# Turning the FFN's input rows: identity products on TensorE replaced by 16-bit halves turned by DMA and summed on POOL, with a new order of an SSD chunk's steps

## The chip, the core and the metric

One core of a Trainium2 chip runs the whole layer in one launch. TensorE (PE) multiplies, DVE (VectorE), ACT (ScalarE) and POOL (GpSimd) do the elementwise work, SP (SyncE) issues nearly all DMAs, in the order of its queue. The metric is the device time of one execution in microseconds (us), lower is better; the median of repeated runs is compared.

## What is computed

One decoder layer on 2048 rows of 1024 numbers (float32):

```python
h = x + rms_norm(W_out @ [SSD(groupA); RWKV7(groupB)], post_mix_norm)   # both read rms_norm(x, pre) @ w_in
hn = rms_norm(h, pre_ffn_norm)
u = causal_conv(hn @ ffn_w_up)                    # 2 x 2816 columns
y = h + rms_norm((silu(gate) * val) @ ffn_w_down, post_ffn_norm)
```

The SSD mixer works in 16 chunks of 128 rows with a state carried from chunk to chunk:

```python
y_diag = (C B^T * decay_in) X ; y_off = C state_in * exp(a_cs) ; state = decay * state + B^T (decay_states X)
y = group_rms_norm((y_diag + y_off + D x) * silu(z)) * norm_g
```

## The kernel before

The program has three phases. Phase R (to about 1010 us) computes the RWKV half and the input products for both halves. Phase S computes the SSD half chunk by chunk, multiplies both halves by `w_out`, adds `x`, writes `h` to memory (`H`), normalises it for the FFN and writes it *transposed* to memory (`HN`, features on partitions, 1024 tokens in each of two tensors). Phase F is the FFN in two halves of 1024 tokens: up products with weights split in two 16-bit halves (a factored form with seven products for eight), convolution, gate and down products. The first half also makes the split weights and stores them to memory (`UW`, `DW`); the second half loads them.

**Who sets the order.** On PE the order is that of the program text throughout. On the other engines and on SP's queue, in phase S and for the FFN's first two column blocks, the framework's scheduler lists the instructions by a simulation of the program. From then on `Program` (L56) writes the order for DVE, ACT, POOL and SP: it keeps a list of operations with an estimated length and the operations they depend on, plays PE's order forward, gives each other operation a due time, and picks on each engine the ready operation that is due first. `Q` is SP's queue. An operation on `Q` that writes no tile of the plan is a store (`UW<-w` L1344, `DW<-dw` L1580, the output rows L1710).

**A round of phase S.** `S_PLAN` is the order of the steps of one round n (1 to 15); `c` is chunk n, `n` chunk n+1, `p` chunk n-1, `q` chunk n-2, `s` and `t` the next pair of chunks, in even and in odd rounds. PE executes them in this order:

- `c.begin` (L947): identity products of X (`px`) and the scores (`psc`); DVE makes `Xdt` and `yt`.
- `c.decay.g` (L978): two products make a bank `bc` from `R` (rows of running decays, fetched by `n.rows`, L974, after `t.flip`, L909, has written them to memory); four ACT exponentials, then DVE and ACT take the rest. There is one `bc` bank.
- `Z` (L931): one quarter of a later chunk's `z` product, 6 matmuls; after the fourth quarter ACT copies the bank (`sz<-z`, L943). There is one such bank. Three `Z` of a round are used in rounds 1 to 12 and four in 13 to 15 (`S_QUOTA`).
- `c.off`, `c.keys`, `c.y`, `c.state`: the state's part `pf` (its scratch on DVE has the tag `sq`), the turned keys `pb`, the chunk's own part `py` with the gate and the norm's squares (scratch `sq`), and the new state `pst`.
- `p.norm` (L1040): four identity products turn the normalised rows (`pY`); ACT and DVE make the two 16-bit halves `Y`.
- `p.o.dh.part` (L1050): 12 matmuls of half `dh` of the output product; part 0 reads `yr` (RWKV's rows), part 1 reads `Y`. After part 1 ACT copies the bank to `m`. There are two `o` banks.
- `q.post.0` and `q.post.1` (L1070): the square of `m` and its root, `m` times the gain, plus `x` on POOL, store to `H`, square and root again, `xi` = normalised rows times the gain (DVE, L1085). Then for each half of 512 features four identity products turn `xi` into a bank `ht` that shares the two `o` banks (L1090), ACT copies it into `hT`, and after the second half one DMA stores `hT` to `HN`. The first half of `hT` serves as scratch for the squares.
- `s.steps`, `t.sums`, `t.flip`: step sizes and running decays of the next pair.

After round 15 the tail (`S_TAIL`) interleaves the last chunks' steps with the FFN's first two column blocks (`F`).

Of the kernel before, what the change touches and what calls it, by code (L numbers as in the profile page):

```python
# [7 lines left out]
F32 = mybir.dt.float32  # L8
F16 = mybir.dt.float16
BF16 = mybir.dt.bfloat16  # L10
AF = mybir.ActivationFunctionType
ALU = mybir.AluOpType
# [5 lines left out]
D = 1024  # L18
P = 128
KT = 8  # L20
# [35 lines left out]
class Program:  # L56

    SHARED = 0.55, 0.75  # L60
    LAG = {"T": 0.25, "V": 0.12, "A": 0.14, "G": 0.12, "Q": 2.0}

    def __init__(self):
        self.on, self.ops, self.writer, self.readers, self.tensor, self.near = False, [], {}, {}, None, set()

    def add(self, engine, us, fn, reads=(), writes=()):
        if not self.on:
            fn()
            return
        n = len(self.ops)  # L70
        before = set()
        for r in reads:
            if r in self.writer:
                before.add(self.writer[r])
            self.readers.setdefault(r, []).append(n)
        for w in writes:
            if w in self.writer:
                before.add(self.writer[w])
            before.update(self.readers.pop(w, ()))
            self.writer[w] = n  # L80
        if engine == "T":
            if self.tensor is not None:
                before.add(self.tensor)
            self.tensor = n
        if engine == "V" and any(r[0] in ("u", "d") for r in reads):
            self.near.add(n)
        before.discard(n)
        self.ops.append((engine, us, fn, before))

    def run(self):  # L90
        ops = self.ops
        count = len(ops)
        after = [[] for _ in ops]
        for n, (_, _, _, before) in enumerate(ops):
            for b in before:
                after[b].append(n)
        due, at = [1e9] * count, 0.0
        for n, (engine, us, _, _) in enumerate(ops):
            if engine == "T":
                due[n] = at  # L100
                at += us
        for n in range(count - 1, -1, -1):
            engine, us, _, _ = ops[n]
            for a in after[n]:
                due[n] = min(due[n], due[a] - us - self.LAG[engine])
        left = [len(o[3]) for o in ops]
        ready = [0.0] * count
        wait = {k: [] for k in self.LAG}
        for n in range(count):
            if not left[n]:  # L110
                wait[ops[n][0]].append(n)

        now, order, busy, coming = 0.0, [], {}, []
        while len(order) < count or busy:
            for k, some in wait.items():
                if k in busy:
                    continue
                some = [n for n in some if ready[n] <= now + 1e-9]
                if some:
                    n = min(some, key=lambda n: (due[n], n))  # L120
                    wait[k].remove(n)
                    order.append(n)
                    busy[k] = [ops[n][1], n]
            rate = dict.fromkeys(busy, 1.0)
            if "V" in busy and "G" in busy and busy["V"][1] not in self.near:
                rate["V"], rate["G"] = self.SHARED
            step = min([v[0] / rate[k] for k, v in busy.items()] + [
                ready[n] - now for k, some in wait.items() if k not in busy for n in some])
            now += step
            for k in list(busy):  # L130
                busy[k][0] -= step * rate[k]
                if busy[k][0] < 1e-9:
                    n = busy.pop(k)[1]
                    for a in after[n]:
                        ready[a] = max(ready[a], now + self.LAG[k])
                        left[a] -= 1
                        if not left[a]:
                            wait[ops[a][0]].append(a)
        for n in order:
            ops[n][2]()  # L140
        self.__init__()


class Space:
# [27 lines left out]
    "Dt", "pp rr ones3 E", "identb mnegb", "Btok", "Xdt", "Xd", "aend dec sgs sgv sgr", "ST0 ST1", "sq", "yt0",  # L172
)
S_RIGHT = (
    "ident_s mhalf_s", "ssm pov por ss pnv pnr", "Y", "yr", "xi", "m", "gpost", "gpre2", "hT", "yt", "wo",
)
F_EARLY = ("us", "s3", "b0", "b1", "b2", "b3")
F_MID = (
# [8 lines left out]
c.decay.1 m.z.2 m.z.3 t.steps u.z.0 u.z.1 u.z.2 n.rows c.y u.z.3 c.state  # L187
"""
S_PLAN = """
c.begin c.decay.0 Z c.off p.norm c.keys Z c.decay.1 p.o.0.0 Z t.sums s.steps p.o.0.1 t.flip Z n.rows q.post.0 c.y c.state  # L190
p.o.1.0 q.post.1 p.o.1.1
"""
S_QUOTA = (3,) * 12 + (4,) * 3
S_TAIL = """
# [46 lines left out]
def bcast_row(tc, K, pool, i, name):  # L241
    t = pool.tile([P, D], F32, name=name)
    tc.nc.scalar.dma_start(t, K.rows[i].partition_broadcast(P))
    return t
# [14 lines left out]
def rsqrt_cols(tc, K, pool, ss, n, scale, eps, name, psum=False, bufs=1):  # L259

    nc = tc.nc
    v = pool.tile([P, n], F32, name=name + "v", tag=name + "v", bufs=bufs)
    r = pool.tile([P, n], F32, name=name + "r", tag=name + "r", bufs=bufs)
    (nc.vector if psum else nc.gpsimd).tensor_scalar(out=v, in0=ss, scalar1=scale, scalar2=eps, op0=ALU.mult, op1=ALU.add)  # L264
    nc.gpsimd.tensor_tensor(out=r, in0=v, in1=K.mhalf[:, :n], op=ALU.pow)  # L265
    return r
# [518 lines left out]
def phase_S(tc, K, x, w_z, w_dt, w_o, XN, XC, YR, H, HN, blocks=8):  # L785
    nc = tc.nc
    V, S, G_ = nc.vector, nc.scalar, nc.gpsimd
    TB = 256
    wk, psp = Space(tc, "s_"), Space(tc, "sp_", space=PSUM)
# [50 lines left out]
    def bank(name, tag, bufs=1):  # L840
        return psp.tile([P, 4, P], F32, name=name, tag=tag, bufs=bufs)
# [81 lines left out]
    class Chunk:  # L923
# [146 lines left out]
        def post(self, part):  # L1070

            m, n = self.m, self.n
            if part == 0:
                ss = wk.tile([P, 1], F32, name="ssm" + self.cf, tag="ssm")
                self.hT = wk.tile([P, KT, P], F32, name="hT" + self.cf, tag="hT")
                jk = self.hT.rearrange("p a b -> p (a b)")[:, 0:D // 2].bitcast(BF16)
                S.activation(jk, m, AF.Square, accum_out=ss)
                r = rsqrt_cols(tc, K, wk, ss, 1, 1.0 / D, EPS, "po")
                V.scalar_tensor_tensor(out=m, in0=m, scalar=r[:, 0:1], in1=gpost, op0=ALU.mult, op1=ALU.mult)
                G_.tensor_tensor(out=m, in0=m, in1=self.xin, op=ALU.add)  # L1080
                K.marks[n] = nc.sync.dma_start(H[n], m)
                ss = wk.tile([P, 1], F32, name="ssh" + self.cf, tag="ss")
                S.activation(jk, m, AF.Square, accum_out=ss)
                r = rsqrt_cols(tc, K, wk, ss, 1, 1.0 / D, EPS, "pn")
                V.scalar_tensor_tensor(  # L1085
                    out=self.xin, in0=m, scalar=r[:, 0:1], in1=gpre2, op0=ALU.mult, op1=ALU.mult)
            ps = (bank(f"ht{self.cf}{part}", "yb") if n >= N - 2 else bank(f"ht{self.cf}{part}", "o", 2))
            for u in range(4):
                kt = 4 * part + u
                nc.tensor.transpose(ps[:, u, :], self.xin[:, kt * P:(kt + 1) * P], K.ident)  # L1090
            S.activation(self.hT[:, 4 * part:4 * part + 4, :], ps, AF.Copy)
            if part == 1:
                nc.sync.dma_start(HN[n // 8][:, :, P * (n % 8):P * (n % 8) + P], self.hT)


    N = 2 * blocks
# [45 lines left out]
    gpost = bcast_row(tc, K, wk, 1, "gpost")  # L1142
    gpre2 = bcast_row(tc, K, wk, 2, "gpre2")
# [759 lines left out]
```

## Time and profile before

| | |
|---|---|
| median of 3 runs (lowest, highest) | 2685.07 us (2680.1, 2686.81) |
| profiled execution | 2684.99 us, its span 2682.6 us |
| mean granted PE clock | 0.972 of full speed |
| busy: PE, DVE, ACT, POOL | 2470.8 (92%), 1925.8 (72%), 1210.7 (45%), 1223.3 (46%) us |
| rounds 2 to 15 of phase S | 1036 to 1376 us |
| tail, FFN's first half, second half | 1376 to 1434, to 2082, to the end |

The span runs from the first to the last instruction of the profiled execution. A busy time is the sum of an engine's instructions. A wait is put down to the instruction that released it; idle time of an engine that is not the bound costs nothing.

### The profile page before, as it was taken

Reading aid. Unit: us, or ns where it says so; the run is one execution under the profiler, and the core shown is the slowest. Engines: PE = TensorE matmul, PEld = TensorE weight load, DVE = VectorE, ACT = ScalarE, POOL = GpSimd, SP = SyncE. Lnnn points to the kernel's source line nnn. Section 1 sums busy time; section 2 is a strip of 40 time slices with the busy share of each in tenths; the row PEclk is TensorE's granted clock in tenths of the full one; section 3 lists DMA queues with packets and bytes.
Section 4 is the critical chain, followed back from the end, with each engine's and each line's share of the span. In section 5 each row is a group of like instructions: output and inputs, shape, how many; then the busy total and the mean of one; then the engine's idle time right before and its main releaser. Section 6 shows DMA issues by size and latency. Waiting matters only on the chain. (4 is left out here: it accounts for less than half of the span.)

```text
span 2682.6 us, 53962 instructions
## 1 busy us (share of the span) xinstructions
PE 2470.8 (92%) x21340; PEld 1554.9 (58%) x21340; DVE 1925.8 (72%) x3655; ACT 1210.7 (45%) x2467; POOL 1223.3 (46%) x1324
## 2 busy tenths in 40 slices
PE   4889999999999988999997999999998999999998
PEld 4778888888888855555543344444433444444443
DVE  7768777777777665567777868787889836565557
ACT  6445555555565453444444543435353333123132
POOL 2344444444545343224467565556657523222135
PEclk8899999999999989999999899999999999999999
DMA  7233222332223253334355444343435643333243
GB/s 211 71 66 71 53 60 58 67 78 53 56 60 71 78 176 110 107 124 136 128 194 169 155 143 153 130 173 114 168 115 192 196 140 100 103 102 102 87 151 112
DMA packets 309341, 310.74 MB, mean 116 GB/s; under 512 B 168160, under 2 KB 213600, under 8 KB 305760
## 3 DMA queue, kind: packets, MB, share of 16 engines
q1 hardware_dynamic: 307792, 305.72, 37.8%
q8 instruction: 167, 2.74, 0.4%
q10 hardware_dynamic: 1296, 1.58, 0.2%
q14 instruction: 86, 0.70, 0.1%
HBM read 187.85 MB, written 110.99 MB: 111 GB/s over the span
## 5 line engine op out<-in xcount | busy, mean ns | idle before, releaser
L1375 PE MATMUL u<-b,w 128*128 128x512 f16 x3696 | 815.2, 383 | 32.2 <-ACT w L1216 15.9
L1375 PEld LDWEIGHTS <-w 128*128 128x128 f16 x3696 | 363.3, 99 | 480.5 <-issue 27.8
L286 PE MATMUL d<-xt,wr 128*128 128x129 f16 x5376 | 336.8, 224 | 17.0 <-DMA xt<-xh 15.3
L1611 PE MATMUL d<-dw,fa 128*128 128x512 f16 x1512 | 336.9, 381 | 12.8 <-DVE dw L1575 10.6
L286 PEld LDWEIGHTS <-wr 128*128 128x128 f16 x5376 | 322.9, 100 | 30.6 <-ACT wr L249 15.3
L1611 PEld LDWEIGHTS <-fa 128*128 128x128 f16 x1596 | 157.2, 98 | 213.5 <-issue 30.5
L1393 DVE TENSOR_TENSOR C<-u,C 128x512 f32<-128x512 f32 x220 | 150.5, 685 | 155.7 <-PE u L1375 148.9
L286 PE MATMUL c<-xt,wc 128*128 128x131 f16 x3072 | 205.2, 227 | 24.1 <-ACT tr L426 10.8
L286 PEld LDWEIGHTS <-wc 128*128 128x128 f16 x3072 | 189.0, 100 | 40.7 <-issue 32.4
L1624 DVE TENSOR_TENSOR acc<-d,acc 128x512 f32<-128x512 f32 x212 | 139.9, 682 | 50.8 <-PE d L1611 50.0
L573 DVE TENSOR_TENSOR tmp<-atl,xl 128x60 f32<-128x60 f32 (+24 forms) x465 | 140.5, 302 | 44.0 <-DMA atl<-ATd 32.5
L1428 DVE SCALAR_TENSOR_TENSOR p<-C,fpar,p 128x1024 f32<-128x1024 f32 x88 | 128.4, 1459 | 60.5 <-ACT p L1424 58.1
L1223 DVE SCALAR_TENSOR_TENSOR w<-us,w 128x512 f16<-128x512 f32 x132 | 121.5, 927 | 53.8 <-ACT w L1216 51.0
L1221 POOL TENSOR_TENSOR fa<-p,fa 128x512 f16<-128x512 f32 x100 | 132.6, 1342 | 58.2 <-ACT fa L1216 58.1
L449 DVE SCALAR_TENSOR_TENSOR ca<-rc,cw,ca 128x128 f32<-128x128 f32 x384 | 132.5, 390 | 25.6 <-POOL ca L444 25.3
L1216 ACT ACTIVATE fa<-p 128x512 f16<-128x512 f32 x110 | 66.5, 626 | 152.6 <-DVE p L1441 125.3
L576 DVE TENSOR_TENSOR xl<-xl,tmp 128x60 f32<-128x60 f32 (+24 forms) x465 | 124.4, 268 | 11.2
L1434 POOL COPY fcarry<-C 128x2 f32<-128x2 f32 x88 | 35.4, 402 | 197.0 <-DVE C L1393 196.9
L1428 DVE SCALAR_TENSOR_TENSOR a<-C,fpar,a 128x1024 f32<-128x1024 f32 x88 | 115.3, 1310 | 7.4 <-ACT a L1424 5.4
L1347 POOL TENSOR_TENSOR us<-us,us 128x512 f32<-128x512 f32 x66 | 101.4, 1536 | 41.2 <-DMA us<-in_w_u_dram 20.7
L1389 ACT ACTIVATE C<-u 128x512 f32<-128x512 f32 x88 | 51.9, 590 | 143.7 <-PE u L1375 126.4
L1216 ACT ACTIVATE w<-us 128x512 f16<-128x512 f32 x132 | 80.0, 622 | 78.1 <-POOL us L1347 57.1
(316 smaller groups left out, 4495.5 us busy)
## 6 DMA issues: line engine op xcount, KB each, us to landing
UW<-w SPq DMA_DIRECT2D x154, 256.0 KB
w<-UW SPq DMA_DIRECT2D x154, 256.0 KB
us<-in_w_u_dram SPq DMA_DIRECT2D x88, 256.0 KB
DW<-dw SPq DMA_DIRECT2D x70, 256.0 KB
dw<-DW SPq DMA_DIRECT2D x56, 256.0 KB
hs<-HN SPq DMA_DIRECT2D x48, 256.0 KB
r<-in_w_d_dram SPq DMA_DIRECT2D x10, 1024.0 KB
xin<-in_x_dram SPq DMA_DIRECT2D x16, 512.0 KB
```

Source lines behind the costliest of these rows:

```text
L286: nc.tensor.matmul(ps, w[:, a, kt, :], xt[:, b, kt, cols], start=n == 0, stop=n == 3 * KT - 1)
L449: V.scalar_tensor_tensor(out=acc[:, q], in0=raw[:, q, k:k + 128], scalar=cw[:, g + q, k:k + 1], in1=acc[:, q], op0=ALU.mult, op1=ALU.add)
L573: chain.tensor_tensor(out=tmp[:, :m, :n], in0=atl[:, j, j + 1:32].unsqueeze(1).to_broadcast([P, m, n]), in1=xl[:, :m, j:j + 1].to_broadcas ...
L576: chain.tensor_tensor(out=xl[:, :m, j + 1:32], in0=xl[:, :m, j + 1:32], in1=tmp[:, :m, :n], op=ALU.add)
L1216: S.activation(h, src, AF.Copy, **({} if scale is None else {"scale": scale}))
L1221: {"V": V, "G": G_}[engine].tensor_tensor(out=l, in0=src, in1=h, op=ALU.subtract)
L1223: V.scalar_tensor_tensor(out=l, in0=src, scalar=scale, in1=h, op0=ALU.mult, op1=ALU.subtract)
L1375: nc.tensor.matmul(bk[at], self.w[i][:, u, k, :], self.half.b[i][:, k, v, :], start=start and n == 0, stop=n == 11, skip_group_check=True)
L1393: op("V", .61, lambda: V.tensor_tensor(out=part(j, x), in0=bk[at], in1=part(*a), op=ALU.add), (("u", 4 * s + at), (*(c0, c1)[a[0]], a[1])) ...
L1428: V.scalar_tensor_tensor(out=o[j], in0=C[j][:, 2 - d:1026 - d], scalar=cw[:, g, 2 - d:3 - d], in1=o[j], op0=ALU.mult, op1=ALU.add)
L1611: nc.tensor.matmul(bk[s, t], pairs[m].a[i][:, u, t * P:t * P + P], pairs[m].w[n][0][:, v, :], start=new and m == 0 and u == v == 0, stop=m ...
L1624: V.tensor_tensor(out=acc[j][:, t], in0=bk[s, t], in1=acc[j][:, t], op=ALU.add)
```

## The change

`post` no longer uses PE. For each half of 512 features ACT converts `xi` to 16 bits (`hl`), DVE subtracts that from `xi` and leaves the 16-bit rest in `xi`'s own place, two DMAs from SP's queue transpose both halves into `tu`, POOL adds them to float32 (`hT`, now half as large), and one DMA stores that half to `HN`. The squares' scratch becomes the tag `sq` (in the last two chunks `yt`). The steps of a round have a new order: `c.off` follows the first decay, two `Z` stand side by side, `q.post.0` follows the second decay and `q.post.1` follows `t.sums`, and `c.y` and `c.state` move behind `p.o.1.0`. In the planner a store becomes ready 4 us later than what it waits for.

```diff
+    STORE = 4.0
     LAG = {"T": 0.25, "V": 0.12, "A": 0.14, "G": 0.12, "Q": 2.0}
...
+        if engine == "Q" and not writes:
+            self.far.add(n)
...
-                        ready[a] = max(ready[a], now + self.LAG[k])
+                        ready[a] = max(ready[a], now + self.LAG[k] + self.STORE * (a in self.far))
...
-    "ident_s mhalf_s", "ssm pov por ss pnv pnr", "Y", "yr", "xi", "m", "gpost", "gpre2", "hT", "yt", "wo",
+    "ident_s mhalf_s", "ssm pov por ss pnv pnr", "Y", "yr", "xi", "m", "gpost", "gpre2", "hT", "hl", "tu", "yt", "wo",
...
 S_PLAN = """
-c.begin c.decay.0 Z c.off p.norm c.keys Z c.decay.1 p.o.0.0 Z t.sums s.steps p.o.0.1 t.flip Z n.rows q.post.0 c.y c.state
-p.o.1.0 q.post.1 p.o.1.1
+c.begin c.decay.0 c.off Z Z c.decay.1 Z q.post.0 p.norm Z c.keys p.o.0.0 t.sums q.post.1 s.steps p.o.0.1 t.flip n.rows
+p.o.1.0 c.y c.state p.o.1.1
 """
...
-                self.hT = wk.tile([P, KT, P], F32, name="hT" + self.cf, tag="hT")
-                jk = self.hT.rearrange("p a b -> p (a b)")[:, 0:D // 2].bitcast(BF16)
+                jk = wk.tile([P, D], BF16, name="jk" + self.cf, tag="sq" if n < N - 2 else "yt", bufs=1 if n < N - 2 else 2)
...
-            ps = (bank(f"ht{self.cf}{part}", "yb") if n >= N - 2 else bank(f"ht{self.cf}{part}", "o", 2))
-            for u in range(4):
-                kt = 4 * part + u
-                nc.tensor.transpose(ps[:, u, :], self.xin[:, kt * P:(kt + 1) * P], K.ident)
-            S.activation(self.hT[:, 4 * part:4 * part + 4, :], ps, AF.Copy)
-            if part == 1:
-                nc.sync.dma_start(HN[n // 8][:, :, P * (n % 8):P * (n % 8) + P], self.hT)
+            cs = slice(512 * part, 512 * part + 512)
+            hi = wk.tile([P, 512], F16, name=f"hl{self.cf}{part}", tag="hl", bufs=2)
+            S.activation(hi, self.xin[:, cs], AF.Copy)
+            lo = self.xin[:, 512 * part:512 * part + 256].bitcast(F16)
+            V.tensor_tensor(out=lo, in0=self.xin[:, cs], in1=hi, op=ALU.subtract)
+            tu = wk.tile([P, 2, 4, P], F16, name=f"tu{self.cf}{part}", tag="tu")
+            nc.sync.dma_start_transpose(tu[:, 0], hi)
+            nc.sync.dma_start_transpose(tu[:, 1], lo)
+            hT = wk.tile([P, 4, P], F32, name=f"hT{self.cf}{part}", tag="hT")
+            G_.tensor_tensor(out=hT, in0=tu[:, 0], in1=tu[:, 1], op=ALU.add)
+            nc.sync.dma_start(HN[n // 8][:, 4 * part:4 * part + 4, P * (n % 8):P * (n % 8) + P], hT)
```

## Rows read from the trace of the kernel before

**Rows 1.** Busy time by stretch: us, each engine (instructions), granted clock, DMA share, GB/s

```profile
1036.00:1222.00 186.00, 177.95 (x1069) 103.43 (x1068) 115.39 (x230) 78.80 (x220) 60.25 (x72) 1.00 0.35 115
1222.00:1376.00 154.00, 143.57 (x780) 80.82 (x779) 112.92 (x175) 73.61 (x194) 73.34 (x76) 0.96 0.46 148
1376.00:1434.00 58.00, 49.45 (x224) 23.04 (x222) 46.22 (x41) 28.41 (x47) 42.47 (x35) 0.91 0.60 201
1434.00:2082.00 648.00, 598.37 (x2682) 264.06 (x2681) 536.40 (x606) 291.19 (x456) 394.92 (x327) 0.97 0.44 150
```

**Rows 2.** PE in order of time, one odd round: start, us, line, out<-in [idle before]

```profile
1105.78 0.60 PE L955 MATMUL px<-ident_s,xbc 128*128 128x128 f32 x4
...
1109.46 0.60 PE L1045 MATMUL pY<-ident_s,yt 128*128 128x128 f32 x4
...
1116.08 2.75 PE L1065 MATMUL o<-wo,Y 128*128 128x512 f16 x12
...
1120.06 0.66 PE L1090 MATMUL ht<-ident_s,xi 128*128 128x128 f32 x4 [1.12 <-DVE xi L1085]
...
1120.55 1.90 PE L1015 MATMUL py<-Xdt,Dt 128*128 128x64 f32 x16
...
1125.79 0.60 PE L1090 MATMUL ht<-ident_s,xi 128*128 128x128 f32 x4
...
1126.23 2.75 PE L1065 MATMUL o<-wo,Y 128*128 128x512 f16 x12
...
1128.82 0.60 PE L955 MATMUL px<-ident_s,xbc 128*128 128x128 f32 x4
...
1129.70 0.38 PE L982 MATMUL bc<-mnegb,identb 128*128 128x512 bf16 x1
```

**Rows 3.** PE's waits, 980 to 1440: for whom, total us, times, longest

```profile
PE ht L1090 <- DVE xi L1085: 18.4, 12, 5.8
...
PE z L937 <- ACT sz L943: 1.7, 2, 1.0
```

**Rows 4.** PE in order of time behind the waits at 1262, 1365, 1427

```profile
1263.24 3.06 PE L1015 MATMUL py<-Xdt,Dt 128*128 128x64 f32 x16
...
1267.90 4.08 PE L1065 MATMUL o<-wo,yr 128*128 128x512 f16 x12
...
1365.82 3.21 PE L1015 MATMUL py<-Xdt,Dt 128*128 128x64 f32 x16
...
1368.83 4.81 PE L1065 MATMUL o<-wo,yr 128*128 128x512 f16 x12
...
1426.92 1.09 PE L1090 MATMUL ht<-ident_s,xi 128*128 128x128 f32 x4 [5.83 <-DVE xi L1085]
```

**Rows 5.** Groups by line, 1036 to 1376: shapes, count | busy us, mean ns

```profile
L1079 DVE SCALAR_TENSOR_TENSOR m<-m,por,gpost 128x1024 f32<-128x1024 f32 x14 | 30.9, 2207 | 18.6 <-POOL por L265 18.6
...
L1085 DVE SCALAR_TENSOR_TENSOR xi<-m,pnr,gpre 128x1024 f32<-128x1024 f32 x14 | 18.0, 1285 | 19.5 <-POOL pnr L265 19.5
...
L1048 DVE TENSOR_TENSOR Y<-pY,Y 128x512 f16<-128x512 f32 x14 | 9.5, 677 | 0.0
...
L1008 POOL TENSOR_TENSOR yt<-yt,of 128x512 f32<-128x512 f32 x14 | 18.3, 1308 | 0.0
...
L1216 ACT ACTIVATE b<-hs 128x512 f16<-128x512 f32 x17 | 10.6, 627 | 13.2 <-POOL hs L1190 6.9 <-DMA hs<-HN 6.4
```

**Rows 6.** SP's queue in order of time, phase R: a transpose and XN's store

```profile
476.05 1.23 SPq L397 DMA_TRANSPOSE xt<-xin  x1
...
479.40 1.25 SPq L398 DMA_DIRECT2D XN<-xt  x1
```

**Rows 7.** SP's queue in the round of rows 2

```profile
1122.48 0.62 SPq L976 DMA_DIRECT2D R<-rows  x2
```

**Rows 8.** Waits, 1434 to 2200: SP's queue, then POOL: total us, times, longest

```profile
SPq L1344 <- DVE w L1223: 262.0, 121, 10.2
...
POOL us L1347 <- DMA us<-in_w_u_dram: 19.1, 4, 5.9
```

More of the change, by code (lines that the diff above doesn't have):

```diff
@@ L60 @@
     SHARED = 0.55, 0.75
+    STORE = 4.0
     LAG = {"T": 0.25, "V": 0.12, "A": 0.14, "G": 0.12, "Q": 2.0}
     def __init__(self):
-        self.on, self.ops, self.writer, self.readers, self.tensor, self.near = False, [], {}, {}, None, set()
+        self.on, self.ops, self.writer, self.readers, self.tensor, self.near, self.far = False, [], {}, {}, None, set(), set()
     def add(self, engine, us, fn, reads=(), writes=()):
```

## The prediction

> **What bounds the kernel now.** I read the stretches first. In the SSD rounds (1036 to 1376 us of the span) the TensorE matmul row is busy 177.95 of 186 and 143.57 of 154 us, while DVE, ACT and POOL are busy 39 to 73% [rows 1]; so a round lasts as long as its PE work and PE's waits. Then I read one round in order of time [rows 2]: from 1105.78 to 1128.82, 23.04 us, PE has one wait worth the name, 1.12 us ahead of the first `ht` group (`q.post.0`, the identity products that turn `xi`). The list of PE's waits says the same of the whole phase: `ht` waited for `xi` (DVE, L1085) 12 times, 18.4 us, and nothing else reaches 7 us [rows 3]; 5.83 of the 18.4 is one wait at 1426.92, in the tail [rows 4]. Last I looked for what follows a wait: after those at 1262 and 1365 the same matmuls run slower (`py` 3.06 and 3.21 against 1.90 us, `o` 4.08 and 4.81 against 2.75 [rows 2, 4]), the granted clock of that stretch being 0.96 instead of 1.00 [rows 1]: PE is at the lower of its two levels for a few us. The FFN's first half (1434 to 2082) is not free of waits either: PE is idle 648 - 598.4 = 49.6 us there [rows 1].
>
> **What goes.** (a) Each chunk loses two `ht` groups. One takes PE 0.44 us, start to start (1125.79 to 1126.23 [rows 2]). Rounds 2 to 15 hold 14 chunks: 28 x 0.44 = 12.3 us. (b) The waits for `xi` inside the rounds: 18.4 - 5.83 = 12.6 us. (c) The slow matmuls behind them: 1.16 + 1.33 + 1.31 + 2.06 = 5.9 us [rows 2, 4]. (d) In the tail two more chunks (4 x 0.44) and the 5.83 us: 7.6 us. But there POOL is busy 42.5 and DVE 46.2 of 58 us [rows 1], the FFN's first products wait for what these make, and POOL gets four more sums; I count 3 us of the 7.6 (from -5, the four sums on the path, to 7.6).
> Nothing on PE waits for the turned rows any more: HN is read by the FFN's loads rounds later, so what is late next is not HN but the steps that the new order puts closer together.
>
> **What comes, off PE.** Per half: one ACT conversion (0.63 us, L1216, the same form [rows 5]) in place of the ACT copy out of PSUM, so nothing; one DVE subtraction (0.68, as L1048); one POOL sum (1.31, as L1008); two transposes by DMA, each half as wide as those of phase R, whose issue takes 1.23 us on SP and which had landed by 2.1 us after it (476.05 + 1.23 to 479.40 [rows 6]). On DVE that is 28 x 0.68 = 19 us in the rounds, on POOL 37 us. A DVE pass beside a POOL sum is longer: L1079 takes 2.21 where L1085, of the same shape, takes 1.29 [rows 5], and 28 x 0.92 = 26 us more would come so. DVE is idle 70.6 + 41.1 us in the rounds [rows 1] and takes it, but with less room for what is due: (g) +2 us, from 0 to 10. The squares' scratch moves from `hT` to `sq`, so the first square waits for `c.off`'s POOL sum instead of HN's store; with `c.off` earlier that is about 1 us later, on ACT, off the path.
> The Trainium skill's VectorE: DVE Perf Modes (The three transpose paths; rules for kernel authors) speaks against the move: it has 1309 ns for a 128x128 turn by DMA and 390 ns on TensorE, and says to use TensorE where PSUM will do. By it a chunk's 16 blocks would take an estimated 21 us, one after the other, as long as a round. The rows disagree: eight blocks were issued and landed in 3.4 us. The sum goes by the rows.
>
> **The new order.** A round without (a) and (b) is 21.0 us. Three places get tighter.
> (e) `Z Z`: the z bank is one buffer, and in rounds 2, 6 and 10 its first Z ends a chunk's z and the second begins the next. Between the two stood `pf`, `pY`, `pb` (1.5 us), and still PE waited for ACT's copy twice, 1.7 us [rows 3]. Now nothing stands between: 3 x 1.5 = 4.6; with the squares gone from that place on ACT I take 4 (0 to 10, where the third Z of rounds 3, 7 and 11 waits too).
> (f) `p.norm` to `p.o.0.1`: pY started 6.6 us before the product that reads Y (1109.46 to 1116.08). Now `keys`, `o.0.0` and `sums` are between: about 3.4 us in an odd round, 4.0 in an even one with `steps`. The chain is pY 0.60, ACT 0.63, DVE 0.68 = 1.9 us; if DVE has just begun `m` (2.21, L1079), which `q.post.0` now puts right there, 4.1: 0.7 late, in 7 odd rounds 5 us. I take 5 (0, if DVE takes Y first; 15, if a square of 1.06 stands ahead on ACT too, in all rounds).
> (i) `R`: in odd rounds the rows for the next decays go to memory and back on SP's queue. `R` went out 7.2 us before `bc` needed it (1122.48 [rows 7] to 1129.70 [rows 2]); with the 2.05 us of `ht` and wait gone, 5.2 are left, and landing takes about 2.1 [rows 6]. SP gets four transposes and one more store a chunk, 1.23 us each at most; I take 0. The dear case is a rival.
> Two waits are added behind which others stand. POOL's sum waits for a transfer; behind it on POOL is the root for `c.y`'s norm. `py` ended 10 us before the next pY (1120.55 + 1.90 to 1128.82 + 3.68 [rows 2]), now about 9 (a Z and a decay more, an `o` and an `ht` fewer between); its chain of two passes, squares, root and scaling is about 4, so a sum that holds POOL 3 us costs nothing. `tu` is one buffer, so the second pair of transposes waits on SP for the first sum; behind it are `yr`, `x` and, in odd rounds, `R`. both loads are wanted 7 us or later into the next round.
>
> **STORE.** The planner now lets stores of the FFN's weight halves be overtaken for 4 us. SP stood 262.0 us behind L1344's stores in the first half; POOL waited 19.1 us for `us` rows that came late [rows 8]. (h) The products waited mostly while POOL and ACT worked through, so I count 3 us of gain; between +10 (a worse plan) and -19.1 (all of that wait).
>
> **Sum.** -12.3 - 12.6 - 5.9 - 3 + 2 + 4 + 5 - 3 = -25.8 us. The profiled execution took 2684.99 us (span 2682.6), the median is 2685.07: 2659 us.
>
> **Rivals.**
> 1. *More* (2640): PE takes Y and z without a wait (-9) and half of STORE's 19.1 us reaches PE (-10 for the -3). For it: the squares leave ACT's busiest place. Against: PE's waits in the first half end on ACT and DVE, not on a transfer. Chance 0.16.
> 2. *Half* (2674): (e) and (f) at their upper ends, +6 and +10. For it: DVE at 73% in rounds 10 to 15 with two passes more [rows 1]. Chance 0.12.
> 3. *No change* (2680): the rounds gain, but the FFN's first stages are held by POOL and DVE, whose work is as long as before plus the ten sums (13 us) and ten subtractions (7 us) after round 12: +20. For it: POOL 42.5 of 58 us in the tail. Against: its idle 154 - 73.3 us in rounds 10 to 15 [rows 1]. Chance 0.11.
> 4. *Slower* (2690 to 2730): SP's order puts `R` behind the second half's store. `xi` is ready 14.3 us into a round (1105.78 to 1120.06); ACT and DVE 1.3, two issues 2.5, landing 2.1, sum 1.3, and the second pair 2.5 + 2.1 + 1.3: the store goes at 27.4, `R` is there at 29.5, needed at 21.0 + 0.9: 7.6 us late. Behind each such wait PE runs slow for 5.9 / 2 us. Seven odd rounds: 53 + 20 us, 2732; it decides from the third such round on (2659 + 31). For it: `tu` and `hT` have one buffer each. Against: `R` is ready some 4 us before that store. Chance 0.12.
> 5. *Slow turns*: were a chunk's turns as long as a round (21.0 us), `xi` would come free too late for the next `x`, `m` and both `o` banks would stay full, and a round would last as long as the turns and the chain beside them (POOL's `m`, a square, a root, `xi`: about 7 us by rows 5): 14 x 7 - 26 = 72 slower, 2757. Against: rows 6. Chance 0.02. The page above would have it so.
>
> **How the numbers follow.** The forecast (2650 to 2670) has 0.47. Faster by over 0.3% (8 us, about what a measurement here tells from none): 0.47 + 0.16 + 0.12 = 0.75; within: 0.11; slower: 0.12 + 0.02 = 0.14. The range, 2638 to 2692, leaves out the far end of the first rival (0.06) and most of the last two (0.13).
>
> **What would show it.** No `ht` products; a round of about 21.5 us in place of 23.0; clock 1.00 over 1036 to 1350. (e): a wait of `z` for `sz` in rounds 2, 6, 10. (f): `o` waiting for Y on DVE in odd rounds. (i): `bc` waiting for `R`. STORE: L1344's share of SP's waits well below 262 us. It is wrong if the rounds keep 23 us, if PE's wait for `bc` or Y exceeds 20 us in sum, or if the start of the second half moves by less than the rounds gained.

## The result, and the profile after

The changed kernel takes 2690.64 us (median of 11 runs), the one before 2682.75 beside it: ratio 1.0029, 95% interval 1.0017 to 1.0041. It is 8 us slower where 26 faster were forecast. The profiled execution has a span of 2688.9 us at a granted clock of 0.966; before it was 2682.6 at 0.972.

The stretches first: busy time of PE, PEld, DVE, ACT and POOL, granted clock, DMA share, GB/s, of the changed kernel; they answer to [rows 1].

```profile
1036.00:1222.00 186.00, 174.41 (x1007) 97.96 (x1007) 120.35 (x247) 78.18 (x222) 78.13 (x87) 0.98 0.50 137
1222.00:1376.00 154.00, 137.62 (x736) 74.99 (x735) 119.28 (x181) 70.76 (x183) 90.55 (x85) 0.96 0.55 162
1376.00:1434.00 58.00, 43.59 (x185) 18.50 (x184) 48.82 (x45) 29.14 (x51) 45.07 (x39) 0.92 0.65 193
1434.00:2082.00 648.00, 603.88 (x2686) 265.73 (x2685) 524.74 (x606) 290.69 (x459) 394.71 (x327) 0.97 0.45 153
```

In the rounds PE is busy 9.5 us less than before, though the stretch is as long: what PE no longer does has become idle time. POOL has 35 us more, DVE 11, and the DMA share went from 0.35 to 0.50 in the first stretch. The 13 rounds from round 2's first `px` to round 15's take 315.9 us for 311.7 before, 24.3 each, so the rounds kept their length. From the first `px` of round 2 to the FFN's first down product the trace of before has 469.9 us, this one 478.5; the rest of the span differs by 2 us.

PE's waits of the changed kernel, 980 to 1440 (total, times, longest), against [rows 3]:

```profile
PE px L958 <- DVE ST L1041: 12.3, 5, 5.0
PE z L940 <- ACT sz L946: 6.7, 6, 3.4
...
PE u L1381 <- DVE C L1399: 5.6, 1, 5.6
PE o L1068 <- DVE Y L1051: 5.0, 2, 3.8
PE acs L905 <- ACT aend L993: 3.1, 2, 1.7
PE pY L1048 <- DVE yt L1029: 2.6, 2, 1.9
PE dt L873 <- ACT aend L993: 2.5, 4, 1.3
```

The 18.4 us for `xi` are gone, and other waits have come in their place. The largest stands in no list of the prediction: `px` (the products of X that begin a round) waits for DVE's sum of ST (the state). Two places show how waits arise. Round 7, all engines in order of time (start, us, ..., idle before):

```profile
1147.76 1.15 POOL L1098 TENSOR_TENSOR hT<-tu 128x512 f32<-128x512 f16 x1 [7.59 <-DMA tu<-xi]
...
1153.43 1.15 POOL L1098 TENSOR_TENSOR hT<-tu 128x512 f32<-128x512 f16 x1 [3.45 <-DMA tu<-xi]
1154.53 1.26 POOL L1011 TENSOR_TENSOR yt<-yt,of 128x512 f32<-128x512 f32 x1
1155.83 1.06 ACT L1079 ACTIVATE jk<-m 128x1024 bf16<-128x1024 f32 x1 [2.47 <-POOL yt L1011]
...
1156.88 0.58 ACT L946 ACTIVATE sz<-z 128x512 f32<-128x512 f32 x1
...
1157.51 2.72 PE L940 MATMUL z<-ws,xs 128*128 128x512 f16 x6 [3.41 <-ACT sz L946]
```

POOL's sum waits for its transfer, `c.off`'s sum stands behind it, the square waits for that sum (they share the scratch `sq`), ACT's copy of z stands behind the square, and PE's next z behind the copy: 3.41 us, and then z at 2.72 us for six instead of 1.47. Round 10 and the first product of round 11, DVE, POOL and PE:

```profile
1240.92 1.68 POOL L1196 TENSOR_TENSOR ht<-hs,hs 128x512 f32<-128x512 f32 x1
...
1241.40 3.77 DVE L896 SCALAR_TENSOR_TENSOR dq<-dq,de 128x16 f32<-128x16 f32 x4
1242.57 1.15 POOL L1098 TENSOR_TENSOR hT<-tu 128x512 f32<-128x512 f16 x1
...
1243.68 1.25 POOL L1196 TENSOR_TENSOR hs<-ht,hs 128x512 f32<-128x512 f32 x1
...
1248.09 0.68 DVE L1041 TENSOR_TENSOR ST<-pst,ST 128x512 f32<-128x512 f32 x1
...
1248.83 1.11 PE L958 MATMUL px<-ident_s,xbc 128*128 128x128 f32 x4 [4.98 <-DVE ST L1041]
```

Four small passes (0.17 us each where POOL is idle) take 3.77 us, about as long as the row of POOL passes beside them, and ST, for which `px` waits, stands behind them and behind other passes of DVE. Of the three POOL passes only `hT` is new; the other two prepare the FFN's first rows, as they did before. All but 0.6 of `px`'s 12.3 us are four waits from here on (1249 to 1327), where that work runs beside the rounds. The mean of L896 is 341 ns; the same line was at 218 before, but it is at 320 without POOL's sums as well (e7, e14 below). The Trainium skill's SBUF — State Buffer (Who interferes with whom) says that a DVE pass with two inputs in SBUF and a POOL pass that reads SBUF take turns, whole instruction by whole instruction; these rows agree.

The groups of POOL's sums and DVE's subtractions (count | busy, mean ns | idle before), against [rows 5], and a pair of transposes on SP's queue (round 7), against [rows 6]:

```profile
L1098 POOL TENSOR_TENSOR hT<-tu 128x512 f32<-128x512 f16 x26 | 32.5, 1248 | 85.4 <-DMA tu<-xi 73.6 <-issue 11.8
...
L1093 DVE TENSOR_TENSOR xi<-xi,hl 128x512 f16<-128x512 f32 x26 | 19.8, 765 | 1.1 <-ACT hl L1091 1.1
```

```profile
1149.50 1.24 SPq L1095 DMA_TRANSPOSE tu<-hl  x1
1150.84 1.21 SPq L1096 DMA_TRANSPOSE tu<-xi  x1
```

Sums and subtractions last about what was forecast (1.31 and 0.68), and POOL's sum of this pair starts at 1153.43, 1.4 us after the end of the second issue. No single step took so much longer than forecast that it would explain the result.

### The profile page after: what moved, and what is told of

Its sections match the earlier page's. It is cut to its first block, busy times and chain, and to the rows that moved or that the text cites. A ratio compares the mean times of both kernels' runs of the same rounds, so it can differ in the third digit from the quotient of the medians.

```text
span 2688.9 us, 53872 instructions
## 1 busy us (share of the span) xinstructions
PE 2468.3 (92%) x21212; PEld 1548.0 (58%) x21212; DVE 1931.9 (72%) x3687; ACT 1208.2 (45%) x2467; POOL 1262.5 (47%) x1356
## 3 DMA queue, kind: packets, MB, share of 16 engines
q8 instruction: 166, 2.72, 0.4%
## 5 line engine op out<-in xcount | busy, mean ns | idle before, releaser
L289 PEld LDWEIGHTS <-wr 128*128 128x128 f16 x5376 | 325.2, 101 | 31.8 <-ACT wr L252 14.7
L689 POOL TENSOR_TENSOR tS<-S,Pi 64x256 f32<-64x256 f32 x64 | 40.4, 631 | 164.9 <-DVE S L699 162.5
```

Of the source, the lines that this page charges most:

```text
L289: nc.tensor.matmul(ps, w[:, a, kt, :], xt[:, b, kt, cols], start=n == 0, stop=n == 3 * KT - 1)
```

## The experiments

Ratios are to the kernel before on the same chip, with 95% intervals; 1% is 27 us. "To the down product" is the time from round 2's first `px` to the FFN's first down product in the run's one trace (before: 469.9).

| run | us | ratio | to the down product |
|---|---|---|---|
| e1 after, STORE 0 | 2694.07 | 1.0025 [1.0014, 1.0036] | 480.5 |
| e2 before, STORE 4 | 2682.03 | 0.9984 [0.9970, 0.9999] | 466.8 |
| e3 before, new order | 2781.21 | 1.0344 [1.0328, 1.0359] | 567.4 |
| e4 after, old order | 2702.62 | 1.0058 [1.0043, 1.0073] | 488.5 |
| e5 after, own scratch for squares | 2699.23 | 1.0078 [1.0060, 1.0095] | 491.4 |
| e6 after, sums don't wait | 2690.67 | 1.0039 [1.0025, 1.0052] | 482.2 |
| e7 after, no sums | 2671.88 | 0.9967 [0.9953, 0.9981] | 461.7 |
| e8 after, sums later | 2703.21 | 1.0088 [1.0073, 1.0103] | 494.7 |
| e9 before, no turn | 2644.16 | 0.9847 [0.9823, 0.9870] | 430.5 |
| e10 before, free sums | 2703.48 | 1.0069 [1.0046, 1.0091] | 482.5 |
| e11 after, old place of c.state | 2682.70 | 0.9986 [0.9973, 1.0000] | 470.8 |
| e12 before, first ht later | 2669.44 | 0.9939 [0.9918, 0.9960] | 455.8 |
| e13 new order, no turn | 2657.27 | 0.9910 [0.9893, 0.9926] | 444.4 |
| e14 after, no transposes, no sums | 2657.15 | 0.9919 [0.9899, 0.9939] | 450.5 |
| e15 before, tied sums | 2684.36 | 1.0011 [1.0000, 1.0023] | 471.9 |
| e16 e12, STORE, tail | 2667.05 | 0.9952 [0.9935, 0.9969] | 456.1 |
| e17 after, no transposes | 2680.44 | 0.9987 [0.9974, 0.9999] | 466.5 |
| e18 e7 and e11 | 2665.53 | 0.9931 [0.9912, 0.9949] | 453.4 |

**The parts of the change, one at a time.**

e1 and e2:

```diff
-    STORE = 4.0
+    STORE = 0.0
```

> The changed kernel with STORE at 0, the rest unchanged. Theory P (POOL stands at the sums for the transposes, c.off's sum and the squares behind it): STORE has no part, 2689 to 2692 us. Theory S (the planner's delay for stores costs the FFN's first half): 2682 to 2685. If STORE helps as the prediction had it (3 us): 2693 to 2696.

> The kernel before with STORE = 4 alone. Theory P: 2679 to 2685, no change of over 3 us. Theory S: 2688 to 2692. The prediction's own value: 2680; SP's waits behind the UW stores (262 us) should fall by a third or more in either case.

Without `STORE` the changed kernel is the same; alone it takes 4 us off the kernel before, with an interval that all but reaches 1. It moved the stores as meant; SP's waits of the changed kernel, 1434 to 2200, against [rows 8]:

```profile
SPq L1350 <- DVE w L1229: 121.7, 45, 10.1
```

In e1 the same line has 253.7 us. As the time is the same, PE hardly waited for these stores.

e3 and e4 exchange the two orders of S_PLAN and leave the way of the turn.

> The kernel before, identity products on PE kept, with the new order of a round alone. Theory O (the order itself costs: px right behind c.state on one bank, two Z side by side): slower than before by 10 us or more, 2692 to 2705, with px waiting for ST. Theory P: the order alone costs little beside what ht's waits give back, since ht is now asked for later in the round: 2675 to 2685.

> The changed kernel with the old order of a round, turns by DMA kept. Theory O: the gain forecast for the turns is free, 2655 to 2668, px and z wait no more. Theory P: POOL still stands at the sums, ACT's square and z's copy wait behind c.off's sum: 2680 to 2692.

e3's waits of PE, 980 to 1440:

```profile
PE ht L1090 <- DVE xi L1085: 66.1, 13, 5.3
```

The new order puts `ht` where `xi` is never ready, so it can't be had with PE's turn; and the transposes are dearer in the old order (e4, 8 us above the changed kernel). The two parts need each other, and exchanging them prices neither.

**Three attempts to take a wait away.** e5 gives the squares a tile of their own:

```diff
-jk = wk.tile([P, D], BF16, name="jk" + self.cf, tag="sq" if n < N - 2 else "yt", bufs=1 if n < N - 2 else 2)
+jk = wk.tile([P, D], BF16, name="jk" + self.cf, tag="jk")
```

> The changed kernel with a scratch of their own for post's squares (tag jk, one more buffer) in place of sq. Theory P, link by link: POOL's wait for the transposes stays (some 70 us in the rounds), but ACT's square no longer stands behind c.off's sum, so ACT's copy of z and its last exponentials come in time: the waits of z, acs and dt (12.3 us in the changed kernel) and the slow matmuls behind them go, 2674 to 2682 us. If the scratch is not the link (rival: the order's px behind ST alone): 2687 to 2692.

It is slower by 13 us than the changed kernel. PE's waits for z fall from 6.7 to 2.1 us, but `bc` now waits for ACT's `aend`, which was 1.0 us in the changed kernel; of e5's waits of PE, 980 to 1440:

```profile
PE bc L985 <- ACT aend L993: 23.3, 12, 4.2
```

The link of round 7 is real, and taking it away this way gives nothing. What it costs by itself e5 does not show, since another wait came in its place.

e6 lets POOL's sum add ACT's half to itself, so it waits for no transfer (HN holds other numbers):

```diff
-            G_.tensor_tensor(out=hT, in0=tu[:, 0], in1=tu[:, 1], op=ALU.add)
+            G_.tensor_tensor(out=hT, in0=hi.rearrange(...), in1=hi.rearrange(...), op=ALU.add)
```

> The changed kernel with POOL's sum adding the untransposed high half to itself: the transposes are issued as before, POOL does the same work but does not wait for them (left out: the turned halves, so HN holds other numbers). Theory P: POOL's 70 us of waits go, c.off's sum comes in time, 2668 to 2680 us. Rival D (the transposes' load on the DMA queues and SP delays R, yr or x): no change, 2687 to 2692. Rival L (POOL's added work, 42 us, slows DVE beside it): also no change.

The time is the same, though the 73.6 us that POOL stood for the transfers are gone (it still stands 62.0 us ahead of the sums, for `hl` and for the store of the `hT` before). `c.off`'s sum is in time now: ACT's square waits 4.4 us for it where it waited 23.0. But `bc` waits 9.9 us for `R`, 0.8 in the changed kernel. So the wait for the transfers can go without a gain; that it costs nothing where it stands is not shown. e8 goes the other way and moves the sums behind the next round's `c.off`, with two buffers of `tu`:

> The changed kernel with the sums and HN's stores of a chunk moved behind c.off's sum of the next round on POOL, and two buffers for the turned halves, so that the transposes have landed when POOL comes to the sums. Theory P: POOL's wait for the transposes falls from 73.6 us to under 15, z and dt wait no more; px behind ST stays: 2668 to 2682 us. Theory O (px behind ST and z side by side carry the loss): 2685 to 2692.

It is worse by 16 us than the changed kernel: now `R` and `yr` come late. Of e8's waits of PE, 980 to 1440:

```profile
PE bc L986 <- DMA R<-rows: 23.0, 6, 5.4
PE o L1068 <- DMA yr<-YR: 11.7, 1, 11.7
```

Both loads share SP's queue with the stores to HN. A late `R` is what the fourth rival described, in another kernel than the one predicted.

**What leaving out the sums gives.** e7 stores the transposed halves to HN as they are:

```diff
-            hT = wk.tile([P, 4, P], F32, name=f"hT{self.cf}{part}", tag="hT")
-            G_.tensor_tensor(out=hT, in0=tu[:, 0], in1=tu[:, 1], op=ALU.add)
-            nc.sync.dma_start(HN[n // 8][...], hT)
+            nc.sync.dma_start(HN[n // 8][...], tu.rearrange("p v a b -> p (v a b)").bitcast(F32).rearrange(...))
```

> The changed kernel without POOL's sums: HN is stored straight from the two turned halves, the same bytes (left out: the sum, so HN holds the halves side by side). Theory P: as without the wait, 2666 to 2680. Rival L: clearly below that kernel, by 5 us or more, since DVE's passes beside the sums get short. Rival D: no change against the changed kernel, 2687 to 2692.

17 us of the changed kernel go with POOL's sums (19 against e6, whose sums don't wait for the transfers). ACT's wait for `c.off`'s sum, 1036 to 1376, of the changed kernel and of e7, and PE's of e7, 980 to 1440:

```profile
ACT jk L1079 <- POOL yt L1011: 23.0, 13, 3.0
```

```profile
ACT jk L1079 <- POOL yt L1011: 4.4, 10, 0.5
PE px L958 <- DVE ST L1041: 9.0, 5, 3.8
PE z L940 <- ACT sz L946: 3.8, 6, 0.7
PE bc L986 <- DMA R<-rows: 3.7, 4, 1.6
```

The waits for `acs` and `dt`, 5.6 us in the changed kernel, are not in e7's rounds at all. So in the changed kernel the sums reach PE in the rounds mostly through ACT, as in round 7, and through `px`. Of the time to the down product 12 us go in the 13 rounds and 5 behind round 15's start.

**The gain by itself.** e9 leaves PE's `ht` out of the kernel before, with nothing in its place:

```diff
-            ps = (bank(f"ht{self.cf}{part}", "yb") if n >= N - 2 else bank(f"ht{self.cf}{part}", "o", 2))
-            for u in range(4):
-                kt = 4 * part + u
-                nc.tensor.transpose(ps[:, u, :], self.xin[:, kt * P:(kt + 1) * P], K.ident)
+            ps = self.xin[:, 512 * part:512 * part + 512].rearrange("p (a b) -> p a b", b=P)
             S.activation(self.hT[:, 4 * part:4 * part + 4, :], ps, AF.Copy)
```

> The kernel before, its order kept, with PE's identity products for the FFN's rows left out and nothing put in their place (ACT copies xi itself, so HN holds rows that are not turned). It takes the forecast's gain by itself: the terms (a) to (c), -12.3 - 12.6 - 5.9, and up to 7 of the tail, are paid or not, without the new order and without POOL's sums. If the gain side of the forecast was right: 2645 to 2655 us, ratio 0.985 to 0.989, rounds of about 21 us. Rival (PE's 30 us do not set the rounds; the next wait, of DVE, ACT or the z bank, takes their place at once): 2665 to 2680, ratio 0.994 to 0.999, with new waits of PE for px, z or pY of 10 us or more in sum.

41 us faster. Its stretches, as above:

```profile
1036.00:1222.00 186.00, 184.30 (x1115) 106.60 (x1122) 111.57 (x249) 87.73 (x246) 68.99 (x81) 1.00 0.42 130
1222.00:1376.00 154.00, 146.25 (x759) 77.50 (x762) 112.12 (x179) 79.58 (x195) 90.97 (x91) 0.98 0.56 176
```

PE is busy 184 of 186 us; 13 rounds take 277.7 us for 311.7 before, and from there to the down product it is 5 us less. The gain was there.

**What the sums cost on their own.** e10 and e15 add two sums of 128x512 a chunk to the kernel before, in e10 of a constant tile, in e15 of `xi`'s half:

```diff
+            pd = wk.tile([P, 512], F32, name=f"pd{self.cf}{part}", tag="pd")
+            xh = self.xin[:, 512 * part:512 * part + 512]
+            G_.tensor_tensor(out=pd, in0=xh, in1=xh, op=ALU.add)
```

> The kernel before plus two sums of a 128x512 tile on POOL in each chunk, from a scratch tile that is set once into another one that nobody reads; no instruction waits for them but POOL's next. It prices POOL's added work without the transposes, without the new order and without a wait. Theory W (what took the forecast's gain is POOL's work itself, beside DVE and in front of POOL's other work): +12 to +22 us, ratio 1.005 to 1.008, as leaving the sums out of the changed kernel gave 19. Rival (the sums cost only where the new order puts them, ahead of c.off's sum and beside DVE's small passes): within 4 us of before, 0.9985 to 1.0015.

> The kernel before plus one sum of 128x512 on POOL behind each half's ht, that adds xi's half to itself into a scratch tile nobody reads; so each sum stands in its own chunk, unlike in e10. It prices POOL's 32 sums in the old order. Theory W (POOL's work itself, beside DVE and in POOL's queue): +10 to +22 us, ratio 1.004 to 1.008. Rival (a sum costs only where much else is tight, as in the changed kernel): within 5 us, 0.998 to 1.002.

e10 is 18 us slower, but says little: its sums had nothing to wait for, and all of them ran ahead of 1064 us of the span, nine in round 2, in which `ht` waited 7.0 us. That round took 33.6 us for 22.2; the twelve after it took as long as before (289.3 and 289.4). In e15 they follow their own chunk's `xi`, and they cost 3 us, none of it in the 13 rounds (310.4 for 311.7). So the same work can be cheap. e15 keeps PE's `ht` and its waits for `xi`, though (18.3 us), which may cover some of it; no run has the sums in the old order with `ht` gone, so it is not shown that their place alone makes them dear.

**The ladder.** e13 is e9 in the new order. e14 is the changed kernel without transposes and sums: against e13 it has ACT's conversions and DVE's subtractions, and also `STORE`, the new scratch of the squares and two stores a chunk. e17 adds POOL's sums to e14, e7 the transposes, the changed kernel both.

> The kernel before without PE's identity products (as e9: ACT copies xi itself, HN holds rows that are not turned), but in the new order of a round. Against e9 (2644) it prices the new order by itself. Theory O (the order costs what px's and z's waits are worth): 2650 to 2660, ratio 0.987 to 0.991, px waiting for ST some 10 us in the rounds. Rival (the order is free or pays once PE has no ht; the 28 us between e9 and e7 are all DVE's and the transposes'): 2638 to 2647, ratio 0.982 to 0.986.

> The changed kernel without the transposes and without POOL's sums: ACT's conversion and DVE's subtraction stay, the store to HN takes xi's bytes as they are (HN holds other numbers). Against e13 it prices DVE's 32 subtractions, and against e7 (2672) the 64 transposes on SP and in the DMA engines. Theory D (DVE's passes cost): 2664 to 2672, ratio 0.992 to 0.9955, within 5 of e7. Rival T (the transposes cost, by SP's 1.2 us each and by the DMA engines' share): 2650 to 2660, ratio 0.987 to 0.991, within 5 of e13.

> The changed kernel without the transposes: POOL adds the two halves as they are, HN holds rows that are not turned. It is the fourth corner beside e14 (neither, 2657), e7 (transposes alone, 2672) and the changed kernel (both, 2691). Theory P (the sums are dear by their place in the new order, in front of c.off's sum and the roots): 2670 to 2678, ratio 0.996 to 0.999. Rival (they are dear only beside the transposes; alone they cost what they cost in the kernel before, 3 us): 2655 to 2663, ratio 0.990 to 0.993.

By the ratios: new order +17 us, subtractions (with what else sets e14 apart) +2, transposes +13 without the sums and +11 with them, sums +18 without the transposes and +17 with them; each uncertain by 5 to 8, so the +2 is not told from nothing. The costs of transposes and sums add.

The order's cost lies in the rounds: 292.8 us in e13 for 277.7 in e9, where PE hardly waits at all. Of e13's waits of PE, 980 to 1440:

```profile
PE bc L982 <- ACT aend L990: 6.0, 11, 0.8
...
PE px L955 <- DVE ST L1038: 4.9, 3, 1.8
...
PE z L937 <- ACT sz L943: 2.1, 3, 0.7
```

For the sums, set e14's waits and small passes against e17's: PE's from 980 or 1036 to 1440, DVE's from 1036 to 1376; first e14:

```profile
PE px L958 <- DVE ST L1041: 7.9, 5, 3.4
...
PE pY L1048 <- DVE yt L1029: 3.0, 2, 2.2
...
DVE yt L1029 <- POOL sgr L268: 13.8, 10, 1.4
...
L896 DVE SCALAR_TENSOR_TENSOR dq<-dq,de 128x16 f32<-128x16 f32 x42 | 13.4, 320 | 1.0
```

and e17:

```profile
PE px L958 <- DVE ST L1041: 11.8, 6, 4.5
PE pY L1048 <- DVE yt L1029: 6.3, 2, 5.9
...
DVE yt L1029 <- POOL sgr L268: 22.7, 10, 3.8
...
L896 DVE SCALAR_TENSOR_TENSOR dq<-dq,de 128x16 f32<-128x16 f32 x42 | 18.1, 430 | 1.0
```

The root for `c.y`'s norm (`sgr`) stands behind a sum on POOL, and DVE's `yt` waits longer for it; the small passes are longer beside one more POOL pass, and ST and then `px` are later. Without any sum they are at 320 ns in e14 already, for 174 in e13. In the 13 rounds `px` is the wait that grows most, and the rounds take 304.2 us for 296.3. PE's waits for `pY` all stand behind round 15's start, and so does the other half of the price (162.3 us to the down product for 154.2), in which the FFN's first up products wait longer too. In e17 ACT's square waits only 4.4 us for `c.off`'s sum, as in e7, and the sums are as dear: the price did not hang on the link of round 7. In e15 little of this happens: DVE waits 14.7 us for `sgr` (15.2 before), the small passes are at 173 ns (218 before), and `px` waits 2.2 us.

**px.** e11 puts `c.y` and `c.state` back ahead of `p.o.1.0`; e18 does so without the sums:

```diff
-p.o.1.0 c.y c.state p.o.1.1
+c.y c.state p.o.1.0 p.o.1.1
```

> The changed kernel with c.y and c.state back ahead of p.o.1.0, as the old order had it, so that a product of 2.75 us more stands between pst and the next px, which share one PSUM bank. Theory X (px's wait for DVE's sum of ST, 12.3 us in 5 rounds of the stretch read, comes from that place): the wait goes to under 3 us and the time falls by 6 to 14 us, ratio to before 0.998 to 1.001. Rival (py, now two products earlier, waits for Xd instead, or DVE is late by the same amount elsewhere): px's wait goes and another of 8 us or more comes, time as the changed kernel, 1.002 to 1.005.

> The changed kernel without POOL's sums (as e7: HN is stored straight from the transposed halves) and with c.y and c.state ahead of p.o.1.0 (as e11). If px's wait and the sums are two costs that add, the 8 us of e11 come off e7's 2672: 2660 to 2667, ratio 0.992 to 0.995. Rival (with the sums gone px's wait has room, and the old place costs as much elsewhere): 2669 to 2675, ratio 0.9955 to 0.998.

e11's waits of PE, 980 to 1440:

```profile
PE bc L985 <- ACT aend L993: 7.1, 4, 2.5
...
PE px L958 <- DVE ST L1041: 0.3, 1, 0.3
```

`px`'s 12.3 us go, 6 come back for `aend`, and the time falls by 11 us; e18 is 10 us faster than e7. So it is a cost of its own, that of one place in the new order, with the sums or without. The wait is there without any turn (4.9 us in e13) and grows with what the turn adds (7.9 in e14, 12.3 in the changed kernel). In e18 the next in line shows: `bc` waits 6.6 us for `R`, in 6 waits.

**The cheap version.** e12 moves one thing in the kernel before: the first half's `ht` behind `c.y` and `c.state`; the chain that makes `xi` stays.

```diff
 c.begin ... n.rows q.post.0 c.y c.state
-p.o.1.0 q.post.1 p.o.1.1
+q.turn.0 p.o.1.0 q.post.1 p.o.1.1
```

> The kernel before with one thing moved: the first half's identity products (ht) stand behind c.y and c.state in PE's order (3.0 us later), the chain that makes xi stays where it was. Everything stays on PE. If the wait for xi is what can be had cheaply: the 12.6 us of waits in the rounds go to under 2 and the slow clock behind them (5.9) too, -12 to -18 us, 2664 to 2671, ratio 0.993 to 0.9955. Rival (the second ht, the o banks or HN's store become late instead): 2678 to 2690, with PE's waits for ht or o above 8 us.

> The kernel before with ht behind c.y and c.state (e12), STORE as in the change (e2), and in the tail the chains of the last two chunks one to three groups of FFN products earlier and their ht one group behind them. PE keeps the turn. By the rows of e12: 7.2 + 2.3 us of waits in the tail go, and e2's 4 us come off: 2654 to 2662, ratio 0.989 to 0.992. Rival (the FFN's first products wait for ACT and DVE in place of ht, and STORE gives nothing here): 2665 to 2671, as e12.

`q.turn.0` is `ht` and ACT's copy of it. e12 is 16 us faster than the kernel before and 24 than the changed one. Its stretches:

```profile
1036.00:1222.00 186.00, 180.69 (x1113) 106.87 (x1120) 119.84 (x235) 80.86 (x228) 62.79 (x76) 1.00 0.38 123
1222.00:1376.00 154.00, 145.87 (x789) 81.28 (x792) 116.04 (x180) 76.19 (x190) 86.47 (x87) 0.99 0.52 167
```

`ht` waits for `xi` only in round 15 and in the tail (8.6 us in 2 waits), the clock of the second stretch is 0.99 where it was 0.96, and in the 13 rounds, which take 298.2 us, no wait of PE is longer than 2.1 us. e16 adds `STORE` and an earlier tail; it was forecast at 2654 to 2662 and is no faster than e12.

## Why the prediction was wrong

- **(a) to (d), the gain, was right**, and a little small: 34 us counted, 41 ± 6 measured (e9). In the trace 34 us go in the 13 rounds, where (a) to (c) counted 31, and 5 behind them, where (d) counted 3. The bound was read well: a round lasts as long as PE's work and waits.
- **(g), DVE and POOL, is the step that failed.** It took 2 us (0 to 10) for all of the added work, since DVE is idle 112 us of the rounds. DVE's subtractions may be worth that (+2, not told from nothing, e14). POOL's sums cost 17 (e7) to 18 (e17). The prediction asked how much longer the passes would be, and for POOL's wait for a transfer, but not enough which pass stands behind: ACT's square behind `c.off`'s sum, and ST behind the small passes. Idle time on an engine is no cover for work in front of a pass on which PE waits next. Which wait carries the price differs between the changed kernel and e17; that the sums are dear is shown by leaving them out, the path by the waits alone.
- **The cost of the transposes, 0, was wrong too**: +13 (e7 against e14). That they take 1.2 us of issue and land about when forecast was right, and (i) as written as well (`R` 0.8 us late in sum). Of the 11 us in the traces up to the down product, 7.5 fall in the 13 rounds, where `R` is late by 3.7 us in e7 and `px` waits 1.7 us more. The rest I could not divide: `R` and `yr` come late in some of the variants, and the DMA share is 0.50 where it was 0.35. What of the 13 us is SP's order and what the DMA engines was not tried.
- **The sum left out a wait**: `px`, `pst` and `pb` share one PSUM bank, and the new order leaves one product of 2.6 us between `pst` and `px`, into which DVE's sum of ST must fit: 12.3 us of waits, 11 us of time (e11). The prediction looked at three places that get tighter and missed this fourth. In the round of [rows 2] an `o`, an `ht` and another `o` stand between `pst` and `px`, of which [rows 2] has the last two; the others:

```profile
1122.29 1.08 PE L1035 MATMUL pst<-Xd,Btok 128*128 128x256 f32 x4
1123.20 2.75 PE L1065 MATMUL o<-wo,yr 128*128 128x512 f16 x12
```

- **(e)** said 4 for z: 6.7 us of waits for 1.7 before, of which 3.4 in round 7, by way of POOL. That was near. **(f)** said 5 for Y: the 5.0 us are one wait of 1.2 in round 15 and one of 3.8 in the tail, where the kernel before had 2.7, and none in the other odd rounds; the number was met by luck. The order as a whole is 17 (e13 against e9), of which the traces have 14 ahead of the first down product. Besides `px` and z it is `bc`, which waits for ACT's `aend` in 11 places of e13: no term of the sum.
- **(h) STORE** said 3: in the kernel before 4 (e2), in the changed one nothing (e1).
- **Scratch of the squares, about 0**: the link exists (23.0 us of ACT's waits for POOL's sum), and the run with a tile of its own is slower (e5).
- **The wait for the transfers, 0 if it holds POOL 3 us**: it held POOL up to 7.6 us, and a kernel without it is as slow (e6), with `R` late instead.
- The fourth rival had the sign for another reason: not `R` behind the store, but POOL's sums, the transposes and the order. The third rival placed POOL's sums in the FFN's first stages, at 20 us; half of what the sums cost in e17 against e14, 8 of 16 us, falls behind round 15's start.

By ratios, in us: -41 (no `ht`), +17 (order), +2 (subtractions), +13 (transposes), +17 (sums) = +8. This must come to the measured difference, as each term is the step from one kernel of the ladder to the next; e17 alone tests that two of them add. `px` is part of the order's term and of the later ones.

## What to carry to other kernels

A wait of the bounding engine is often had for a change of place: here 16 of the 41 us came by putting four matmuls some 3 us later, while the whole change, with its move to engines with idle time, gave all 41 back and 8 more. Work that moves to an engine with idle time is priced by what stands behind it in that engine's queue and by who waits for that, not by the idle share. After every reordering, go through the shared buffers again: which two users of one bank or scratch tile have come closer together.

## What the runs showed of the hardware

- The issue of a DMA transpose takes 1.2 us on SP's queue at 128x512 as at 128x1024 (1.24 and 1.21 us here, 1.23 in [rows 6]): halving the width left the issue as long, and two in place of one held the queue twice as long.
- Beside a row of three POOL passes (1.68, 1.15 and 1.25 us) three small DVE passes with two inputs each lasted until one of them ended: 3.77 us for four passes that take 0.17 us alone.
